# Attention of a decoder trunk: scores of the next pair of heads placed inside the products of this pair, and the output projection split 2, 3, 3 instead of 2, 2, 4

## The chip, the cores and the metric

The kernel runs on one core of a Trainium2 chip. The time is in device microseconds (us) of one execution. The engines work side by side and each carries out its own instructions in a fixed order: PE multiplies matrices and writes its results to eight banks of an accumulator memory (PSUM), DVE does elementwise work and scans, ACT does copies, casts and functions such as the sigmoid, POOL does a little setup, and SP's queue issues the loads. The order on each engine is fixed when the program is built.

## The reference, cut to what matters

A trunk of two layers works on 512 tokens with 16 learned meta tokens in front (528 rows) and a width of 1024. Layer 0 mixes tokens by causal pooling. Layer 1 uses stick-breaking attention with 16 heads of 64. Each mixer is followed by a dense feed-forward part (SwiGLU, width 2816), and a norm ends the trunk. The change is in the attention of layer 1:

```python
def _sb_attend(qs, qpos, kvs, kpos):
    z = jnp.einsum('bqhd,bkhd->bhqk', q, k) * (HEAD_DIM ** -0.5)
    mask = kpos[None, :] < qpos[:, None]
    log_keep = jnp.where(mask, log_sigmoid(-z), 0.0)
    later = lax.cumsum(log_keep, axis=3, reverse=True) - log_keep
    a = jnp.where(mask, exp(log_sigmoid(z) + later), 0.0)
    return jnp.einsum('bhqk,bkhd->bqhd', a, v)

def sb_mixer(h, w_qkv, w_o):
    q, k, v = ...   # h @ w_qkv, in 16 heads
    o = sweep_queries(_sb_attend, (q,), (k, v))
    return o.reshape(B, L, N_HEADS * HEAD_DIM) @ w_o
```

So the weight of a key is sigmoid(z) times the product of sigmoid(-z) over all later keys that the query sees.

## The kernel before, in words

**Precision.** Every float32 product is made of three matmuls (`mm3`, line 102): each operand is split into a high part (a cast on ACT) and a low part (a subtraction on DVE), and high x high, high x low and low x high are added up. `wsplit` (line 82) does that for weights, 512 columns at a time. `wraw` (line 75) loads them through SP's queue into six buffers. The split weights have eight buffers each for high and low.

**Units of the attention.** The 16 heads go in 8 pairs, a pair filling the 128 rows of a tile. For pair p there are these steps:

- `proj(p)` (line 498): five half steps, q (512 columns at once), k in two halves of 264 columns, v in two halves. Each is 24 matmuls. Line 524 scales the result with the norm on DVE, and `parts_of` (line 528) splits q and k.
- `values` (line 535): transposes of v on PE, and their split into `vv`.
- `scores` (line 551): three groups of matmuls `z` with masks added (line 570). Query block 3 goes first, then blocks 0 and 1, then block 2 and the start of block 3. All four causal blocks of the pair's two heads lie in strips of 1344 columns, `sg` and `kp`, of which there is one each. Two sigmoids on ACT (line 573) fill them group by group. Then, for each head, a scan on DVE (line 576) makes the running product from the last key backwards in place, and line 578 multiplies it with `sg`. The second head's two instructions are kept behind the first head's.
- `turned(p, hd)` (line 585): ten transposes of the strip on PE (line 589), one for the meta columns (line 602), then the splits `a1`, `a2` and `a0` on ACT and DVE (lines 607 to 614). `a1` and `a2` have room for one head (high and low), and `a0` is one tile.
- `attend(p, hd)` (line 618): nine matmuls `po` of the weights with `vv`, collected into `of`. `finish(p)` (line 636) splits `of` into `os`.
- `wo(p0, p1)` (line 642): the output projection over pairs p0 to p1 in eight steps, one for each chunk of 128 output columns. A step is a weight split, 3 matmuls of 512 columns for each pair (`pw`), and an addition to the residual stream `hT` on DVE (line 655).

**The loop.** For each pair, lines 664 to 697 write down: the scores of pair p, its `values`, q and the first half of k of pair p+1, the transposes of head 0, the second half of k, the products of head 0, the transposes of head 1, the first half of v, the products of head 1, the second half of v. For pairs 3 to 6 some steps of `wo(0, 2)` follow. Pair 7 has five steps of `wo(2, 4)` in place of projections. The other three stand between the steps of `wo(4, 8)` at the end (line 699), each of which is followed by a chunk of the next feed-forward part's norm.

**What sets the order.** This written order is a priority. The builder (line 777) lays the instructions of each engine on a timeline of its own estimates and takes, at each moment, the first written one that it believes ready and for which a buffer is free. `tc.issue_after(x)` holds every instruction inside it that runs on x's engine behind x. Before, it holds the scores of pair p behind the last product of pair p-1.

**Banks.** In this stage PSUM has four single banks (tag `one`: projections, a part of the transposes, products, output steps, and the norm's sum of `norm_bcast`, line 164, which takes two) and two double banks (tag `two`: scores, the larger part of the transposes, `values`, and for pair 0 also the projections).

Of the kernel before, what the change touches and what calls it, by code (L numbers as in the profile page):

```python
# [7 lines left out]
F32 = mybir.dt.float32  # L8
# [42 lines left out]
def trunk(ctx: ExitStack, tc: tile.TileContext, x, meta, x_t, gain, pool_w, w_qkv, w_o, w_gate, w_up, w_down,  # L51
# [50 lines left out]
    def mm3(outs, wh, wl, xh, xl, start, stop, more=False):  # L102

        for i, (w, xx) in enumerate(((wh, xh), (wh, xl), (wl, xh))):
            for o, sl in outs:
                nc.tensor.matmul(o, lhsT=w, rhs=xx[:, sl], start=start and i == 0, stop=stop and i == 2,  # L106
                                 skip_group_check=more)
# [377 lines left out]
    with tc.tile_pool(name="att", bufs=1) as ap, phase("ps2", one=4, two=2):  # L485
# [12 lines left out]
        def proj(p):  # L498

            got = {}  # L500
            first = {}

            def half(i, hf):
                if hf == 0:
                    got["w"] = wsplit(wraw(w_qkv[i * KC + p], f"r{'qkv'[i]}{p}"), f"w{'qkv'[i]}{p}")
                    got[i] = blk(f"qf{p}_{i}")
                wh, wl = got["w"]
# [43 lines left out]
        def scores(p, q, k):  # L551


            (qh, ql), (kh, kl) = q, k
            sg, kp = (ap.tile([P, 2, STRIP], F32, tag=t, name=f"{t}{p}", bufs=1) for t in ("sg", "kp"))

            for o, n, regs in ((832, 512, ((3, 0, META, L),)), (0, 416, ((0, 0, 0, 144), (1, 144, 0, 272))),
                               (416, 416, ((2, 0, 0, 400), (3, 400, 0, META)))):
                tz = ps(f"z{p}_{o}", "two", 2)
# [7 lines left out]
                for d in DIAG:  # L567
                    if o <= d < o + n:
                        for hd in range(2):
                            nc.tensor.matmul(tz[:, hd, d - o:d - o + P], lhsT=masks[:, 2], rhs=masks[:, 0], start=False,  # L570
                                             stop=True, skip_group_check=True)
                for dst, sc in ((kp, -1.0), (sg, 1.0)):
                    nc.scalar.activation(dst[:, :, o:o + n], tz[:, :, 0:n], AF.Sigmoid, scale=sc)  # L573

            def weights(hd):
# [5 lines left out]
            with tc.issue_after(weights(0)):  # L581
                weights(1)
            return sg[:, 0], sg[:, 1]
# [52 lines left out]
        def finish(p, of):  # L636
            a, b = (ap.tile([P, SEQ], F32R, tag="os", name=f"os{p}{n}", bufs=11) for n in "hl")
            nc.scalar.copy(a, of)
            nc.vector.tensor_tensor(out=b, in0=of, in1=f32(a), op=ALU.subtract)
            osp[p] = (a, b)  # L640

        def wo(p0, p1):
# [4 lines left out]
            def step(c):  # L647
# [5 lines left out]
                for j in range(n):  # L653
                    mm3([(pj, slice(0, SEQ))], wh[j], wl[j], *osp[p0 + j], j == 0, j == n - 1)
                nc.vector.tensor_tensor(out=hT[c][:, TOK], in0=pj, in1=hT[c][:, TOK], op=ALU.add)

            return [lambda c=c: step(c) for c in range(KC)]

        NP = NH // 2
        got, steps, values = proj(0)  # L660
        for st in steps:
            st()
        early = wo(0, 2)
        for p in range(NP):
            of = ap.tile([P, SEQ], F32, tag="of", name=f"of{p}", bufs=1)
            extra = []
            if p < NP - 1:
                nxt, nsteps, nvalues = proj(p + 1)
                before = []
                fill = nsteps[0:1], nsteps[1:2], nsteps[2:3], nsteps[3:4], nsteps[4:]  # L670
                if p == NP - 2:
                    late, fill = nsteps[3:], fill[:3] + ([], [])
                if 3 <= p < NP - 1:
                    extra = early[:4] if p == NP - 2 else early[:2 if p == 3 else 1]
                    early = early[len(extra):]
            else:
                w = wo(2, 4)
                before, fill = late, (w[0:1], w[1:2], w[2:3], w[3:4], w[4:5])
            with tc.issue_after(last) if p else nullcontext():
                s0, s1 = scores(p, got["q"], got["k"])  # L680
            for st in before:
                st()
            values()
            for st in list(fill[0]) + list(fill[1]):
                st()
            w0 = turned(p, 0, s0)
            for st in fill[2]:
                st()
            attend(p, 0, w0, got["v"], of)
            w1 = turned(p, 1, s1)  # L690
            for st in fill[3]:
                st()
            last = attend(p, 1, w1, got["v"], of)
            finish(p, of)
            for st in list(fill[4]) + list(extra):
                st()
            got, values = nxt, nvalues
# [83 lines left out]
```

## Time and profile before

| what | value |
|---|---|
| three runs | 1085.02, 1086.45, 1087.53 us; median 1086.45 |
| the profiled execution | 1087.54 us, of which 1085.6 us is the span of the trace; mean granted PE clock 0.978 |
| PE busy | 1030.8 us (95%) |
| DVE busy | 856.2 us (79%) |
| ACT busy | 558.2 us (51%) |
| attention | from 410.4 us (first q projection) to 723.4 us (last output step) of the span |

PE is busy nearly everywhere. Its clock is shown as a share of full speed, and it can fall to a half, in which case a busy PE does half as much. So a stage has to be read in three columns: PE's busy time, its clock, and what ended its idle time. The attention is the stage in which PE's busy share is lowest: in slices 18 to 26 of the page's 40 it reads 7 to 9 tenths.

### The profile page before, as it was taken

To read this page: it belongs to the slowest core of one execution; us is meant where nothing else is said; L and a number is where in the kernel's file an instruction comes from. 1 tells how busy PE (TensorE), PEld (TensorE's weight loads), DVE (VectorE), ACT (ScalarE), POOL (GpSimd) and SP (SyncE) were. 2 spreads that over 40 slices of the span, in tenths; PEclk is the share of its full clock that TensorE was granted. 3 is DMA by queue.
4 is the path that set the end of the run, shared out by engine and by line. 5 is a ranking of instruction groups with operands and counts; after the bars stand their busy time and mean duration, and the time that the engine had idled before them with its cause. 6 is when DMAs were issued, how large, how long until landed. Compare 5 with 4: busy or idle time off the path is not lost.

```text
span 1085.6 us, 18620 instructions
## 1 busy us (share of the span) xinstructions
PE 1030.8 (95%) x7302; PEld 956.6 (88%) x7302; DVE 856.2 (79%) x1529; ACT 558.2 (51%) x1131; POOL 6.2 (1%) x16
## 2 busy tenths in 40 slices
PE   8998999999999999798888899799999999999997
PEld 6997999999999998787788778678899999999985
DVE  7899987878888685766688768789987777878855
ACT  7555644545444454555554545356664454455544
POOL 1000000000000010000000000000000000000000
PEclk9999999999999999899999999899999999999999
DMA  9112332233232332101110102222233232333312
GB/s 346 65 53 73 133 98 98 98 98 98 98 97 98 117 108 88 39 30 40 49 59 21 49 30 79 78 97 69 77 105 101 98 98 97 108 107 117 98 39 78
DMA packets 43111, 95.72 MB, mean 88 GB/s; under 512 B 3328, under 2 KB 20096, under 8 KB 43024
## 3 DMA queue, kind: packets, MB, share of 16 engines
q1 hardware_dynamic: 42272, 93.40, 25.9%
q8 instruction: 57, 0.93, 0.3%
q10 hardware_dynamic: 752, 1.14, 0.3%
q14 instruction: 30, 0.25, 0.1%
HBM read 92.43 MB, written 2.10 MB: 87 GB/s over the span
## 4 chain that ended last, share of the span: by engine, by line
PE 80%; DVE 15%; ACT 2%; issue 1%; DMA 1%; SPq 0%; ACTq 0%; DVEq 0%
PE pb L106 15%; PE pd L106 11%; PE pd L330 11%; PE pj L106 11%; PE pa L106 10%; PE pc L106 10%; DVE kp L576 3%; PE pw L106 2%; PE po L628 2%; PE pp L106 2%; PE z L564 2%; PE t L589 2%; DVE sg L578 1%; DVE xl L389 1%; ACT kp L573 1%
## 5 line engine op out<-in xcount | busy, mean ns | idle before, releaser
L576 DVE TENSOR_TENSOR_SCAN kp<-kp,estrip 128x1344 f32<-128x1344 f32 x16 | 47.3, 2954 | 21.0 <-ACT kp L573 21.0
L303 DVE TENSOR_TENSOR h<-pd,h 128x264 f32<-128x264 f32 x96 | 41.2, 431 | 13.9 <-PE pd L106 13.9
L92 ACT CAST ws_3h<-rgate 128x512 fp32r<-128x512 f32 x38 | 23.6, 621 | 55.3 <-PE pb L106 49.3
L589 PE MATMUL t<-consts,sg 128*128 128x128 f32 x160 | 26.1, 319 | 25.5 <-DVE sg L578 22.4
L92 ACT CAST ws_5h<-s 128x512 fp32r<-128x512 f32 x38 | 23.6, 621 | 47.0 <-PE pb L106 36.3
L589 PEld LDWEIGHTS t<-consts,sg 128*128 128x128 f32 x160 | 21.7, 163 | 28.1 <-issue 24.2
L106 PE MATMUL pa<-xl,ws_0h 128*128 128x264 f32 (+1 forms) x152 | 43.4, 285 | 3.2 <-DVE xl L389 3.2
L432 DVE TENSOR_TENSOR u<-pb,m 128x264 f32<-128x264 f32 (+1 forms) x38 | 16.3, 430 | 38.1 <-PE pb L106 38.0
L92 ACT CAST ws_4h<-s 128x512 fp32r<-128x512 f32 x38 | 23.6, 621 | 42.3 <-PE pa L106 25.6
L106 PE MATMUL pb<-xl,ws_1h 128*128 128x264 f32 (+1 forms) x152 | 43.1, 284 | 1.0 <-DVE xl L389 1.0
L106 PE MATMUL pc<-xh,ws_2l 128*128 128x264 f32 (+1 forms) x152 | 43.2, 284 | 0.0
L106 PE MATMUL pb<-xh,ws_1h 128*128 128x264 f32 (+1 forms) x152 | 43.2, 285 | 0.0
L106 PE MATMUL pa<-xh,ws_3h 128*128 128x264 f32 (+1 forms) x152 | 43.1, 284 | 0.0
L106 PE MATMUL pa<-xh,ws_0l 128*128 128x264 f32 (+1 forms) x152 | 43.1, 284 | 0.0
L106 PE MATMUL pb<-xh,ws_6l 128*128 128x264 f32 (+1 forms) x152 | 43.1, 283 | 0.0
L106 PE MATMUL pa<-xl,ws_3h 128*128 128x264 f32 (+1 forms) x152 | 43.0, 283 | 0.0
L106 PE MATMUL pb<-xh,ws_4l 128*128 128x264 f32 (+1 forms) x152 | 43.0, 283 | 0.0
L106 PE MATMUL pc<-xl,ws_2h 128*128 128x264 f32 (+1 forms) x152 | 43.0, 283 | 0.0
L106 PE MATMUL pc<-xl,ws_5h 128*128 128x264 f32 (+1 forms) x152 | 43.0, 283 | 0.0
L106 PE MATMUL pb<-xl,ws_6h 128*128 128x264 f32 (+1 forms) x152 | 43.0, 283 | 0.0
L106 PE MATMUL pc<-xh,ws_2h 128*128 128x264 f32 (+1 forms) x152 | 43.0, 283 | 0.0
L106 PE MATMUL pb<-xl,ws_4h 128*128 128x264 f32 (+1 forms) x152 | 43.0, 283 | 0.0
(1179 smaller groups left out, 4177.6 us busy)
## 6 DMA issues: line engine op xcount, KB each, us to landing
rgate<-in_ffn_w_gate_dram SPq DMA_DIRECT2D x44, 512.0 KB, 3.5
rup<-in_ffn_w_up_dram SPq DMA_DIRECT2D x44, 512.0 KB, 3.4
rd<-in_ffn_w_down_dram SPq DMA_DIRECT2D x42, 512.0 KB, 3.6
rq<-in_sb_w_qkv_dram SPq DMA_DIRECT2D x8, 512.0 KB, 3.4
rk<-in_sb_w_qkv_dram SPq DMA_DIRECT2D x8, 512.0 KB, 3.4
rv<-in_sb_w_qkv_dram SPq DMA_DIRECT2D x8, 512.0 KB, 3.5
h<-in_x_t_dram SPq DMA_DIRECT2D x8, 264.0 KB, 6.8
x<-in_x_dram SPq DMA_DIRECT2D x4, 512.0 KB, 5.4
```

What stands on the lines that cost most here:

```text
L92: nc.scalar.copy(hi, v[:, j:j + w])
L106: nc.tensor.matmul(o, lhsT=w, rhs=xx[:, sl], start=start and i == 0, stop=stop and i == 2, skip_group_check=more)
L303: nc.vector.tensor_tensor(out=hv, in0=pd, in1=hv, op=ALU.add)
L330: nc.tensor.matmul(pd, lhsT=hid[j][x_][:, ts], rhs=w_[:, sl], start=r > 0 and i + j == 0, stop=j == len(hid) - 1 and i == 2, skip_group_ch ...
L389: nc.vector.tensor_tensor(out=xl[i][:, m, :], in0=o, in1=f32(xh[i][:, m, :]), op=ALU.subtract)
L432: tt(out=u[:, a], in0=pb, in1=m1, op=ALU.add)
L564: nc.tensor.matmul(tz[:, hd, c:c + k1 - k0], lhsT=qq[hs, i * P:(i + 1) * P], rhs=kk[hs, k0:k1], start=j == 0 and c == 0, stop=False, skip_ ...
L573: nc.scalar.activation(dst[:, :, o:o + n], tz[:, :, 0:n], AF.Sigmoid, scale=sc)
L576: nc.vector.tensor_tensor_scan(kp[:, hd, ::-1], kp[:, hd, ::-1], estrip[:, ::-1], 1.0, op0=ALU.mult, op1=ALU.max)
L578: return nc.vector.tensor_tensor(out=sg[:, hd, 0:STRIP - 1], in0=sg[:, hd, 0:STRIP - 1], in1=kp[:, hd, 1:STRIP], op=ALU.mult).ins
L589: nc.tensor.transpose(o, sg[:, c0:c0 + n], ident)
L628: last = nc.tensor.matmul(po[:, i0 * P:512], lhsT=lw, rhs=a, start=t == 0 and j == 0, stop=t == 4)
```

## The change

The helper `mm3` and the steps now return their last matmul, so that others can be placed behind it. `Scores` is the old `scores` cut into its three groups and the scans. `begin` writes them down with given steps in front and between, each held behind the other on PE. In the loop, pair p+1's scores and scans now stand between the transposes of pair p's second head and that head's products, with half a k of pair p+2 in front of the first two groups and the other half in front of the third; q of pair p+2 follows. Both halves of v of pair p+1 and its `values` stand between the transposes and the products of pair p's first head. Pair 0's scores are written down with its own v around, and q and k of pair 1 follow them before the loop. All projections use single banks. The output projection runs over pairs 0 and 1 (four steps after each of pairs 4 and 5), over pairs 2 to 4 (in place of projections in pairs 6 and 7), and over pairs 5 to 7 at the end. `os` has 10 buffers in place of 11.

```diff
@@ mm3
-                nc.tensor.matmul(o, lhsT=w, rhs=xx[:, sl], start=start and i == 0, stop=stop and i == 2,
-                                 skip_group_check=more)
+                last = nc.tensor.matmul(o, lhsT=w, rhs=xx[:, sl], start=start and i == 0, stop=stop and i == 2,
+                                        skip_group_check=more)
+        return last.ins
@@ proj
-                    got["w"] = wsplit(wraw(w_qkv[i * KC + p], f"r{'qkv'[i]}{p}"), f"w{'qkv'[i]}{p}")
+                    got["w", i] = wsplit(wraw(w_qkv[i * KC + p], f"r{'qkv'[i]}{p}"), f"w{'qkv'[i]}{p}")
...
-                if p == 0:
-                    if hf == 0:
-                        first[i] = ps(f"pj{p}_{i}", "two", 2)
-                    pj = first[i][:, hf, :n]
-                else:
-                    pj = ps(f"pj{p}_{i}{hf}", "one")[:, :n]
+                pj = ps(f"pj{p}_{i}{hf}", "one")[:, :n]
                 for k in range(KC):
-                    mm3([(pj, sl)], wh[k], wl[k], uh[k], ul[k], k == 0, k == KC - 1)
+                    last = mm3([(pj, sl)], wh[k], wl[k], uh[k], ul[k], k == 0, k == KC - 1)
...
+                return last
@@ scores
-        def scores(p, q, k):
...
+        class Scores:
+            GROUPS = ((832, 512, ((3, 0, META, L),)), (0, 416, ((0, 0, 0, 144), (1, 144, 0, 272))),
+                      (416, 416, ((2, 0, 0, 400), (3, 400, 0, META))))
+            def __init__(self, p, q, k):
+                self.p, self.q, self.k = p, q, k
+                self.sg = ap.tile([P, 2, STRIP], F32, tag="sg", name=f"sg{p}", bufs=1)
+                self.kp = ap.tile([P, 2, STRIP], F32, tag="kp", name=f"kp{p}", bufs=1)
+            def group(self, g):
+                (qh, ql), (kh, kl) = self.q, self.k
+                o, n, regs = self.GROUPS[g]
+                tz = ps(f"z{self.p}_{o}", "two", 2)
...
+                for dst, sc in ((self.kp, -1.0), (self.sg, 1.0)):
                     nc.scalar.activation(dst[:, :, o:o + n], tz[:, :, 0:n], AF.Sigmoid, scale=sc)
+                return last.ins
+            def weights(self, hd):
...
+            def both(self):
+                with tc.issue_after(self.weights(0)):
+                    self.weights(1)
@@ finish
-            a, b = (ap.tile([P, SEQ], F32R, tag="os", name=f"os{p}{n}", bufs=11) for n in "hl")
+            a, b = (ap.tile([P, SEQ], F32R, tag="os", name=f"os{p}{n}", bufs=10) for n in "hl")
@@ the loop
+        def begin(p, got, before, between):
+            sc = Scores(p, got["q"], got["k"])
+            mark = None
+            for st in before:
+                mark = st()
+            with tc.issue_after(mark) if mark else nullcontext():
+                sc.group(0)
+                mark = sc.group(1)
+            for st in between:
+                with tc.issue_after(mark):
+                    mark = st()
+            with tc.issue_after(mark):
+                sc.group(2)
+            sc.both()
+            return sc.sg
+
         got, steps, values = proj(0)
-        for st in steps:
+        for st in steps[:3]:
             st()
-        early = wo(0, 2)
+        sg = begin(0, got, [], steps[3:4])
+        steps[4]()
+        values()
+        nxt, steps, values = proj(1)
+        for st in steps[:3]:
+            st()
+        early, w = wo(0, 2), wo(2, 5)
         for p in range(NP):
             of = ap.tile([P, SEQ], F32, tag="of", name=f"of{p}", bufs=1)
...
+            v = got["v"]
+            w0 = turned(p, 0, sg[:, 0])
+            for st in steps[3:] if p + 1 < NP else w[4:6]:
+                st()
+            if p + 1 < NP:
+                values()
+            attend(p, 0, w0, v, of)
+            w1 = turned(p, 1, sg[:, 1])
+            got = nxt
+            if p + 2 < NP:
+                nxt, steps, values = proj(p + 2)
+                fill = steps[1:2], steps[2:3], steps[0:1]
+            elif p + 2 == NP:
+                fill = w[0:1], w[1:2], w[2:4]
             else:
...
+                fill = [], [], w[6:8]
+            if p + 1 < NP:
+                sg = begin(p + 1, got, fill[0], fill[1])
             for st in fill[2]:
                 st()
...
+            attend(p, 1, w1, v, of)
+            if p in (4, 5):
+                for st in early[4 * (p - 4):4 * (p - 3)]:
+                    st()
             finish(p, of)
...
         norms[1] = Norm(24, "f1")
-        for c, st in enumerate(wo(4, NP)):
-            if c < 3:
-                w[5 + c]()
+        for c, st in enumerate(wo(5, NP)):
             st()
             norms[1].chunk(c)
```

More of the change, by code (lines that the diff above doesn't have):

```diff
@@ L500, in proj @@
             got = {}
-            first = {}
             def half(i, hf):
                 if hf == 0:
-                    got["w"] = wsplit(wraw(w_qkv[i * KC + p], f"r{'qkv'[i]}{p}"), f"w{'qkv'[i]}{p}")
+                    got["w", i] = wsplit(wraw(w_qkv[i * KC + p], f"r{'qkv'[i]}{p}"), f"w{'qkv'[i]}{p}")
                     got[i] = blk(f"qf{p}_{i}")
-                wh, wl = got["w"]
+                wh, wl = got["w", i]
                 f = got[i]
@@ L569, in scores @@
                         for hd in range(2):
-                            nc.tensor.matmul(tz[:, hd, d - o:d - o + P], lhsT=masks[:, 2], rhs=masks[:, 0], start=False,
-                                             stop=True, skip_group_check=True)
-                for dst, sc in ((kp, -1.0), (sg, 1.0)):
+                            last = nc.tensor.matmul(tz[:, hd, d - o:d - o + P], lhsT=masks[:, 2], rhs=masks[:, 0],
+                                                    start=False, stop=True, skip_group_check=True)
+                for dst, sc in ((self.kp, -1.0), (self.sg, 1.0)):
                     nc.scalar.activation(dst[:, :, o:o + n], tz[:, :, 0:n], AF.Sigmoid, scale=sc)
-            def weights(hd):
+                return last.ins
+            def weights(self, hd):
+                kp, sg = self.kp, self.sg
                 nc.vector.tensor_tensor_scan(kp[:, hd, ::-1], kp[:, hd, ::-1], estrip[:, ::-1], 1.0, op0=ALU.mult,
@@ L579, in weights @@
                                                in1=kp[:, hd, 1:STRIP], op=ALU.mult).ins
-            with tc.issue_after(weights(0)):
-                weights(1)
-            return sg[:, 0], sg[:, 1]
+            def both(self):
+                with tc.issue_after(self.weights(0)):
+                    self.weights(1)
         def turned(p, hd, sg):
@@ L653, in step @@
                 for j in range(n):
-                    mm3([(pj, slice(0, SEQ))], wh[j], wl[j], *osp[p0 + j], j == 0, j == n - 1)
+                    last = mm3([(pj, slice(0, SEQ))], wh[j], wl[j], *osp[p0 + j], j == 0, j == n - 1)
                 nc.vector.tensor_tensor(out=hT[c][:, TOK], in0=pj, in1=hT[c][:, TOK], op=ALU.add)
+                return last
             return [lambda c=c: step(c) for c in range(KC)]
         NP = NH // 2
+        def begin(p, got, before, between):
[13 more added lines that the diff above has]
+            return sc.sg
@@ L660, in trunk @@
         got, steps, values = proj(0)
-        for st in steps:
+        for st in steps[:3]:
             st()
-        early = wo(0, 2)
+        sg = begin(0, got, [], steps[3:4])
[5 more added lines that the diff above has]
+        early, w = wo(0, 2), wo(2, 5)
         for p in range(NP):
             of = ap.tile([P, SEQ], F32, tag="of", name=f"of{p}", bufs=1)
[L666 to L675, printed above, removed]
-            else:
[L677 to L686, printed above, removed]
```

13 lines of the change are left out of this document (removed).

## The prediction

> **What bounds the kernel now.** I read the page first. The tensor engine (PE) is busy almost all of the span, and one group of its instructions, the transposes of the attention weights on line 589, has nearly all of the engine's listed idle time in front of it, released by DVE's product on line 578.
>
> ```profile
> span 1085.6 us, 18620 instructions
> PE 1030.8 (95%) x7302; PEld 956.6 (88%) x7302; DVE 856.2 (79%) x1529; ACT 558.2 (51%) x1131; POOL 6.2 (1%) x16
> L589 PE MATMUL t<-consts,sg 128*128 128x128 f32 x160 | 26.1, 319 | 25.5 <-DVE sg L578 22.4
> ```
>
> Next I cut the attention stage with the view of busy time by stretch: from the first projection of pair 0 to its first scores, one stretch per pair (first score to next first score), the end of pair 7, and the rest of the output projection up to the matmul that sums the next norm. Columns: stretch, length, busy time of PE, PE's weight loads, DVE, ACT, POOL, granted PE clock, DMA share, GB/s.
>
> ```profile
> core 0: us, PE busy (x) PEld busy (x) DVE busy (x) ACT busy (x) POOL busy (x), PEclk, DMA share, GB/s
> 410.40:433.08 22.68, 22.68 (x138) 20.32 (x139) 13.16 (x23) 8.70 (x15) 0.00 (x0) 1.00 0.27 88
> 433.08:464.90 31.82, 25.99 (x192) 23.94 (x191) 23.26 (x32) 17.07 (x35) 0.00 (x0) 0.89 0.11 37
> 464.90:497.25 32.35, 28.87 (x205) 26.02 (x205) 24.06 (x34) 16.36 (x34) 0.00 (x0) 0.95 0.12 42
> 497.25:529.59 32.34, 27.48 (x206) 24.40 (x205) 24.08 (x34) 16.35 (x34) 0.00 (x0) 1.00 0.12 41
> 529.59:564.73 35.14, 31.66 (x217) 28.14 (x217) 25.96 (x38) 17.39 (x36) 0.00 (x0) 0.95 0.16 48
> 564.73:598.47 33.74, 30.22 (x212) 26.94 (x211) 25.10 (x35) 16.77 (x35) 0.00 (x0) 0.95 0.10 33
> 598.47:632.20 33.73, 30.29 (x212) 27.07 (x211) 24.04 (x34) 16.35 (x35) 0.00 (x0) 0.95 0.14 45
> 632.20:661.95 29.75, 26.17 (x170) 22.29 (x169) 21.65 (x30) 14.23 (x31) 0.00 (x0) 0.94 0.16 53
> 661.95:695.03 33.08, 27.53 (x166) 22.76 (x167) 26.16 (x38) 15.63 (x34) 0.00 (x0) 0.90 0.20 64
> 695.03:732.66 37.63, 36.73 (x158) 29.36 (x158) 28.37 (x46) 19.21 (x33) 0.00 (x0) 1.00 0.30 98
> sum 322.26, PE 287.64 PEld 251.25 DVE 235.84 ACT 158.05 POOL 0.00; mean PE 28.76 PEld 25.12 DVE 23.58 ACT 15.81 POOL 0.00
> ```
>
> PE is idle for 322.26 - 287.64 = 34.6 us. It also loses time to a lower clock: (1 - clock) x length over the rows gives 3.5 + 1.6 + 0 + 1.8 + 1.7 + 1.7 + 1.8 + 3.3 = 15.4 us. So 50.0 us of this part are not matmul work at full clock; 272.3 us are. A pair without output projection needs about 27.4 us of PE (28.87 less 1.6; 27.48 at full clock) and 24.1 us of DVE, and takes 32.35.
>
> The view of waits names the releasers in the attention stage, and the timeline of pair 3 shows the chain: third group of scores, sigmoid on ACT, scan of head 0 on DVE (line 576), two evacuations that DVE puts between, the product (line 578), the transposes.
>
> ```profile
> PE t L589 <- DVE sg L578: 22.4, 8, 5.3
> PE po L628 <- DVE a L614: 5.2, 7, 0.9
> ```
>
> ```profile
> 537.76 0.28 PE L570 MATMUL z<-masks 128*128 128x128 bf16 x2
> 538.08 0.86 ACT L573 ACTIVATE kp<-z 128x832 f32<-128x832 f32 x1 [2.89 <-PE z L570]
> 538.98 2.96 DVE L576 TENSOR_TENSOR_SCAN kp<-kp,estrip 128x1344 f32<-128x1344 f32 x1 [3.06 <-ACT kp L573]
> 541.85 0.67 DVE L524 TENSOR_TENSOR qf<-pj,r 128x512 f32<-128x512 f32 x1
> 542.43 0.81 DVE L546 TENSOR_TENSOR vv<-pv,vv 128x640 fp32r<-128x640 f32 x1
> 543.16 1.55 DVE L578 TENSOR_TENSOR sg<-sg,kp 128x1343 f32<-128x1343 f32 x1
> 544.86 1.59 PE L589 MATMUL t<-consts,sg 128*128 128x128 f32 x10 [2.63 <-DVE sg L578]
> 552.56 1.45 DVE L614 SCALAR_TENSOR_TENSOR a<-a0h,consts,t 32x128 fp32r<-32x128 f32 x4
> 554.06 0.50 PE L628 MATMUL po<-a,vv 128*128 128x512 f32 x1 [0.85 <-DVE a L614]
> ```
>
> From the end of the scores (538.04) to the transposes is 6.8 us, 5.3 without the two evacuations (1.5 us). Until then PE had 4.2 us of projection to do and waited 2.63. Of the wait's other cost the clock tells: stretches of 3.4 us around this place.
>
> ```profile
> 545.70:549.10 3.40, 3.40 (x18) 3.40 (x16) 3.40 (x5) 1.20 (x2) 0.00 (x0) 0.50 0.00 0
> 549.10:552.50 3.40, 3.40 (x28) 3.31 (x28) 3.40 (x5) 2.06 (x8) 0.00 (x0) 1.00 0.47 154
> 513.20:516.60 3.40, 3.40 (x31) 3.40 (x30) 3.40 (x4) 2.07 (x4) 0.00 (x0) 1.00 0.02 5
> ```
>
> After the wait of pair 3 PE runs for 3.4 us at half clock and loses 1.7 us; after the like wait of pair 2 (third row) it does not. Pair 2 alone of pairs 1 to 6 has clock 1.00 in the table.
>
> **The change part by part.** The chain of waits gives PE's pieces at full clock: start, length, and count.
>
> ```profile
> 531.94 4.91 PE pj L106 x21
> 522.21 2.93 PE pj L106 x24
> 525.14 1.51 PE po L628 x9
> 550.97 1.09 PE t L589 x10
> 561.94 2.79 PE pw L106 x12
> ```
>
> So a q projection (24 matmuls of 512 columns, 0.234 each) is 5.6 us, half a k or v projection 2.9, a head's products 1.5, a head's transposes 1.1, and an output step 0.2325 per matmul: 1.4 us for two pairs, 2.1 for three. No matmul is added or removed, so the 272.3 us stay; what changes are the losses. I price them one by one.
>
> *Wait for the first transposes.* After the third group of scores of pair p+1, the new order has q of p+2 (5.6) and the second head's products of pair p (1.5): 7.1 us against a chain of 6.8. That alone leaves no wait. But nothing holds q back, and the builder orders PE by its own estimates. Before, it put 21 q matmuls between the second and third groups (531.94, 4.91 us). The new order puts half a k there (2.9); I let q fill the other 2.0 us, which is 9 matmuls. Then 15 x 0.234 + 1.5 = 5.0 us of cover are left and the wait is between 5.3 - 5.0 = 0.3 and 6.8 - 5.0 = 1.8; I take 1.3, nearer to the upper end, because DVE did put work between in pair 3. Pairs 1 to 4: 5.2 us. Pairs 5 and 6 get four output steps of 1.4 us in front: 0. Pair 7 has two steps of 2.1 and 1.5 of products, 5.7 against 6.8 or 5.3: 0.8. Together 6.0, bounds 0 and 4 x 1.8 + 1.5 = 8.7.
>
> *Wait for the first head's products.* From the start of the transposes to the last split that the products need, DVE took 9.2 us (544.86 to 554.01: scan and product of head 1 and the splits). The new order covers this with transposes 1.1, v 5.9, v's own transposes 0.5 and eight of nine product matmuls 1.3: 8.8. The wait is 0.4 plus what else DVE must do there; I take 0.6 (0.85 before, with a shorter cover), for 7 pairs 4.2; bounds 0 and 7 x 1.5 = 10.5.
>
> *Half clock.* Before, 2.63 us of wait and 1.1 of transposes cost 1.7 us in most pairs. With 1.3 of wait I take one pair in four of five: 2.1; bounds 0 and 7 x 1.7 = 12. The Trainium skill says, in TensorE: Matmul & The Clock Gate, section HAM oscillation — how this bites in real kernels, that the clock falls only with idle gaps above about 3.4 us. By that rule this term would be 0 and the time 2 us less, but this trace halves the clock after 2.63. The same page, section Part 4: PE-mode transpose, says that transposes do not count as busy in the same way; with them the gap is 3.7, and the trace agrees.
>
> *Start.* The pieces of pair 0's q and k move from the double banks to the four single ones, which the norm's sum also takes two of. q, the sum (two) and half of k fill all four, so the second half of k now waits until line 137 has read the sum, and q's bank comes free only later.
>
> ```profile
> 417.14 1.05 PE L172 MATMUL abp<-ansq,ones 128*128 128x264 f32 x4
> 420.36 0.77 DVE L137 SCALAR_TENSOR_TENSOR abt<-abp,abt 128x264 f32<-128x264 f32 x2
> 422.38 0.69 DVE L524 TENSOR_TENSOR qf<-pj,r 128x512 f32<-128x512 f32 x1
> ```
>
> q and half of k are 8.5 us from 410.4, so PE has work to 419 or so and the bank is there at 421.2: 1.5 us with the sum's own matmuls; bounds 0 (the sum goes earlier) and 5 (the bank is given after q, 423.1, and the clock falls). Behind it on PE stand pair 0's scores, and q of pair 1 has no free bank to run ahead in. Pair 0's own wait (5.3 in the waits, clock 0.89) gets v, q and k of pair 1 in front, 2.9 + 5.6 + 5.9, and goes.
>
> *Pair 7.* Its transposes are followed by two output steps (4.2) and eight product matmuls (1.3): 1.1 + 4.2 + 1.3 = 6.6 against 9.2, a wait of 2.6, less since DVE has no projection to split. The second head's splits have 4.2 more. I take 3.5 in all, bounds 1 and 9 (the last stretch of pair 7 loses 5.6 + 3.3 now).
>
> *End.* Output projection regrouped as 2, 3, 3 pairs:
>
> ```profile
> 695.03:732.66 37.63, 28.13 (x120) 22.18 (x119) 8.89 (x13) 1.00 0.30 98
> rwo<-in_sb_w_o_dram SPq DMA_DIRECT2D x8, 256.0 KB, 2.7
> rwo<-in_sb_w_o_dram SPq DMA_DIRECT2D x4, 512.0 KB, 3.4
> ```
>
> The first row is the projection alone in the last stretch: 28.1 us of PE. After it, 8 steps of 2.1 = 16.8 remain there; 11 us move into pairs 5 to 7, where they are the cover counted above. Finishing pair 7 is hidden by the matmuls of pairs 5 and 6 in the first steps. But DVE's 28.4 us in that stretch shrink only by splits made earlier, to 25 or so, while PE has 16.8 + 8.6 = 25.4. Now they are level, so I leave 2.3 us of loss (0.9 now); bounds 0.9 and 8. The loads of `w_o` stay 12 issues on SP's queue, and those of q, k and v only change their order there. Four of 256 KB and eight of 384 KB meet a DMA share of 0.10 to 0.20: nothing. The splits and additions of the projection stay the same in elements: nothing.
>
> *Sum.* 1.5 + 6.0 + 4.2 + 2.1 + 3.5 + 2.3 = 19.6 us of losses for 50.0: 30.4 less. The profiled execution took 1087.54 (1085.6 of span and 1.9 around it), so it would take 1057.1. The median of the runs shown, 1086.45, lies 1.1 lower: **1056**.
>
> **Rivals.** *B, DVE's queue and the banks become the bound.* The second group of scores needs the double bank of head 1's transposes, which DVE frees after the splits of head 1, and these wait for head 0's products. That circle is: transposes to products 9.2, head 1's splits about 3, second group and mask 1.2, k 2.9, third group 1.2, chain 6.8: 24.3 us, 3 under PE's 27.4. For it: DVE has 24.1 us of work a pair and only a part of it is in the circle (about 12). If half of the rest is served in front, the circle is 30.3, the loss 2.9 a pair, and with half clock in some 3.6: 7 x 3.6 + 1.5 + 3.5 + 2.3 = 32.5, 17.5 less: 1069. Against it: DVE idles 8 us a pair now.
>
> *C, the cover is spent early, and it is slower.* If all 24 q matmuls go in front of the third group, only the products' 1.5 us stand between it and the transposes, and the wait is 6.8 - 1.5 = 5.3, as at pair 0, with 6.8 us at half clock there (3.5 in the row of pair 0; 2.8 taken). With 0.85 for the products that is 9.0 a pair for pairs 1 to 4 and 7, 45; 5 and 6 keep 0.6 each; 45 + 1.2 + 1.5 + 3.5 + 2.3 = 53.5, 3.5 more than now: 1090. It decides from about 20 matmuls on. For it: the 21 in the trace. Against: half a k now stands there.
>
> *D, it does not overlap.* The strips for sigmoids and scan results stay single, so pair p+1's sigmoids wait until pair p's are read. If all of DVE's 24.1 us and the circle's 8.3 us on other engines (transposes, copies, scores, k, sigmoid) run one behind the other, the pair takes 32.4 as now; 7 x 5 + 7.3 = 42 of loss: 1078. Against: the transposes that read the strips come 2.9 us of k before. The Trainium skill says, in Perfetto Trace Analysis, section Identifying Performance Opportunities, that a gap that repeats can mean too few buffers; by that rule reordering would leave it. Here the releaser is DVE's product, data and not a bank, so the trace speaks against it.
>
> *E, better.* No waits but the start and the end: 1.5 + 1 + 0.9 = 3.4, 1040; with a little left, 1044.
>
> **How the numbers follow.** Forecast 0.58 (own range 1047 to 1064), B 0.20, E 0.07, D 0.06, C 0.09. The range 1042 to 1076 takes in the forecast, B and most of E; it leaves out D, C and the edge of E, about 0.18. A change of 0.2% (2.2 us) is about what can be told from none. C lies beyond it; the edge of D gives 0.03 to no change: faster 0.88, same 0.03, slower 0.09.
>
> **What would show it.** Right: line 589's waits on line 578 fall from 22.4 us to about 6, none above 2; the pairs without output steps take 28.5 to 29.5 us; few half-clock stretches in the stage; the order of PE shows a part of q between second and third groups; the sum of the next norm starts near 702. Wrong: a wait above 4 us at the transposes in most pairs (C), waits of the second score group for DVE's split on line 611 (B), pairs still at 32 (D), or a gap of several us before pair 0's second half of k.

## The result, and the profile after

The changed kernel takes 1060.96 us (median of 4 runs, 1059.19 to 1062.80) against 1085.94 us for the kernel before, run beside it: a ratio of 0.9771, with a 95% interval of 0.9758 to 0.9784. It is faster by 25 us. The profiled execution of after is the slowest of the four, 1062.80 us with a span of 1061.0, and 24.7 us below the profiled execution of before.

From the page of after: the span, the busy times, and the group of scans. DVE's idle time in front of the scans, 3.8 us here, was 21.0 us before.

```profile
span 1061.0 us, 18586 instructions
PE 1023.1 (96%) x7302; PEld 949.3 (89%) x7302; DVE 856.6 (81%) x1529; ACT 556.9 (52%) x1131; POOL 6.2 (1%) x16
L581 DVE TENSOR_TENSOR_SCAN kp<-kp,estrip 128x1344 f32<-128x1344 f32 x16 | 47.3, 2954 | 3.8 <-ACT kp L576 3.4
```

The stage by stretch, in the columns of the prediction. The cuts are the first score of each pair; the first row is pair 0's projection, the last runs from pair 7's last products to the sum of the next norm.

```profile
core 0: us, PE busy (x) PEld busy (x) DVE busy (x) ACT busy (x) POOL busy (x), PEclk, DMA share, GB/s
408.83:423.12 14.29, 12.67 (x76) 11.22 (x76) 10.25 (x19) 7.31 (x13) 0.00 (x0) 1.00 0.20 73
423.12:459.74 36.62, 36.61 (x273) 33.98 (x273) 25.28 (x35) 18.36 (x36) 0.00 (x0) 0.95 0.21 72
459.74:488.70 28.96, 27.61 (x204) 24.48 (x205) 24.84 (x35) 16.42 (x33) 0.00 (x0) 1.00 0.16 56
488.70:517.68 28.98, 27.72 (x204) 24.56 (x204) 24.28 (x34) 16.38 (x33) 0.00 (x0) 1.00 0.11 37
517.68:546.65 28.97, 27.74 (x203) 24.57 (x203) 24.27 (x34) 16.38 (x33) 0.00 (x0) 1.00 0.16 55
546.65:574.93 28.28, 27.47 (x203) 24.57 (x203) 23.40 (x34) 15.27 (x33) 0.00 (x0) 1.00 0.12 39
574.93:608.98 34.05, 33.03 (x229) 28.94 (x229) 28.37 (x42) 17.60 (x37) 0.00 (x0) 1.00 0.19 59
608.98:642.33 33.35, 32.17 (x212) 27.45 (x213) 27.83 (x42) 18.31 (x38) 0.00 (x0) 1.00 0.20 67
642.33:674.28 31.95, 28.36 (x151) 23.27 (x152) 25.74 (x36) 14.18 (x30) 0.00 (x0) 0.89 0.15 50
674.28:705.76 31.48, 27.33 (x106) 21.75 (x106) 22.38 (x36) 16.47 (x28) 0.00 (x0) 0.89 0.25 84
sum 296.93, PE 280.71 PEld 244.79 DVE 236.64 ACT 156.68 POOL 0.00; mean PE 28.07 PEld 24.48 DVE 23.66 ACT 15.67 POOL 0.00
```

The stage is 25.3 us shorter (322.26 before). PE is idle for 296.93 - 280.71 = 16.2 us and loses (1 - clock) x length = 1.8 + 3.5 + 3.5 = 8.8 us, 25.0 together for 50.0. The matmul work is 280.71 - 8.8 = 271.9 us, as before (272.3). (Where PE is idle inside a half-clock stretch, this counts the time twice, about 1 us in either kernel.) A pair without output projection takes 28.97 us for 32.35, with PE idle 1.2 to 1.4 us in pairs 1 to 3. The losses that are left sit in the first two rows and the last two.

PE's waits in the stage (total, times, longest) give them names:

```profile
PE pp L106 <- DVE h L660: 4.1, 1, 4.1
PE t L594 <- DVE sg L583: 3.6, 1, 3.6
PE z L567 <- ACT qk_1h L527: 1.6, 1, 1.6
PE po L633 <- DVE a L619: 1.0, 3, 0.4
```

The wait of the transposes (line 594 now) for DVE's product was 22.4 us in 8 waits; one is left, at pair 7. In the pairs before it the chain is covered, as the timeline of pair 2 shows: last mask of the third score group, scan, product, and the transposes without a wait.

```profile
495.02 0.28 PE L573 MATMUL z<-masks 128*128 128x128 bf16 x2
495.11 0.48 PE L106 MATMUL pj<-anuh,wq3h 128*128 128x512 f32 x1
496.41 2.96 DVE L581 TENSOR_TENSOR_SCAN kp<-kp,estrip 128x1344 f32<-128x1344 f32 x1
499.47 1.56 DVE L583 TENSOR_TENSOR sg<-sg,kp 128x1343 f32<-128x1343 f32 x1
500.75 0.39 PE L633 MATMUL po<-a111h,vv 128*128 128x512 f32 x1
502.25 1.25 PE L594 MATMUL t<-consts,sg 128*128 128x128 f32 x10
```

All of pair 3's q (495.11 to 500.75, 5.6 us) and the products of pair 1's second head (1.5) stand behind the third group. The chain ends at 501.03, 1.2 us before PE comes to the transposes.

At pair 7 the cover is spent early. Of the two output steps that are to follow the third group, one and a third stand in front of it, beside the one meant to (644.56 to 649.6), and 2.9 us of work are left for the chain, up to 653.9:

```profile
654.71 0.67 DVE L660 TENSOR_TENSOR h<-pw,h 128x512 f32<-128x512 f32 x1
...
655.76 1.55 DVE L583 TENSOR_TENSOR sg<-sg,kp 128x1343 f32<-128x1343 f32 x1
657.45 2.36 PE L594 MATMUL t<-consts,sg 128*128 128x128 f32 x10 [3.59 <-DVE sg L583]
```

At the end PE has finished the output projection at 691.0, and the first matmul of the next layer waits for DVE's last residual addition, which stands behind splits and chunks of the norm. By the kernel's text this matmul reads only the first chunk of the norm; but the next layer takes a new set of PSUM banks, and that addition is the last to read the old set:

```profile
693.65 0.76 DVE L153 SCALAR_TENSOR_TENSOR f1ul<-h,gains,f1uh 128x528 fp32r<-128x528 f32 x1
694.33 0.68 DVE L660 TENSOR_TENSOR h<-pw,h 128x512 f32<-128x512 f32 x1
695.16 0.77 PE L106 MATMUL pp<-f1uh,wgate0h 128*128 128x512 f32 x1 [4.15 <-DVE h L660]
```

### The profile page after: what moved, and what is told of

It is laid out like the page before. It is cut to its first block, busy times and chain, and to the rows that moved or that the text cites. A ratio compares the mean times of both kernels' runs of the same rounds, so it can differ in the third digit from the quotient of the medians.

```text
span 1061.0 us, 18586 instructions
## 1 busy us (share of the span) xinstructions
PE 1023.1 (96%) x7302; PEld 949.3 (89%) x7302; DVE 856.6 (81%) x1529; ACT 556.9 (52%) x1131; POOL 6.2 (1%) x16
## 4 chain that ended last, share of the span: by engine, by line
PE 78%; DVE 17%; issue 2%; ACT 1%; DMA 1%; SPq 0%; ACTq 0%; DVEq 0%
PE pb L106 15%; PE pd L106 11%; PE pd L331 11%; PE pa L106 10%; PE pc L106 10%; PE pj L106 9%; PE pp L106 4%; DVE kp L581 2%; PE pw L106 2%; PE z L567 2%; DVE xl L390 1%; DVE a L619 1%; PE t L594 1%; DVE t L387 1%; DVE sg L583 1%
## 5 line engine op out<-in xcount | busy, mean ns | idle before, releaser
L106 PE MATMUL pa<-xh,ws_3l 128*128 128x264 f32 (+1 forms) x152 | 43.3, 285 | 0.0
L106 PE MATMUL pa<-xh,ws_0h 128*128 128x264 f32 (+1 forms) x152 | 43.1, 284 | 0.0
L106 PE MATMUL pb<-xh,ws_1l 128*128 128x264 f32 (+1 forms) x152 | 42.9, 283 | 0.0
L106 PE MATMUL pc<-xh,ws_5h 128*128 128x264 f32 (+1 forms) x152 | 42.9, 282 | 0.0
```

Of the source, the lines that this page charges most:

```text
L106: last = nc.tensor.matmul(o, lhsT=w, rhs=xx[:, sl], start=start and i == 0, stop=stop and i == 2, skip_group_check=more)
```

## The experiments

All are edits of the changed kernel, but for the one on the regrouping alone. Each was timed in three rounds against the kernel before, the last three in five.

**Where q stands.** The theory: what stands behind the third score group decides whether PE waits. The rival: the circle of double banks and DVE's queue (the prediction's B) sets the pair.

```diff
-                fill = steps[1:2], steps[2:3], steps[0:1]
+                fill = steps[1:2], steps[2:3] + steps[0:1], []
```

> All 24 matmuls of the next but one pair's q (5.6 us) are put between the second and third score groups, behind half a k, for pairs 1 to 6; nothing is left out. Theory (what stands behind the third group decides): the transposes of pairs 1 to 4 have only the second head's products, 1.5 us, in front of them against a chain of 5.3 to 6.8 us, so PE waits 3.8 to 5.3 us there and loses about 1.7 to 3.4 more at half clock; the pair grows from 29.0 to 34 us or more, the time rises by 20 to 30 us against the changed kernel, to 1081 to 1091 (the prediction's rival C says 1090). Pairs 5 and 6 keep four output steps and stay. Rival (the circle of double banks and DVE's queue sets the pair, and q's place does not): the pair stays under 30.5 us and the time under 1068.

Measured: 1089.97 us, ratio to before 1.0034 (1.0020 to 1.0049). The whole gain is gone and 0.3% more. The waits, and the stretches behind the first two of them:

```profile
PE t L594 <- DVE sg L583: 22.5, 5, 4.8
```

```profile
475.50:482.30 6.80, 4.79 (x22) 4.82 (x23) 6.77 (x6) 2.21 (x6) 0.00 (x0) 0.50 0.00 0
...
509.60:516.50 6.90, 4.81 (x23) 4.84 (x24) 6.87 (x6) 2.21 (x6) 0.00 (x0) 0.51 0.00 0
```

There are four waits of 4.8 us (the fifth, 3.1, is pair 7's). The last 2.0 to 2.5 us of each and the 4.3 to 4.8 us of work behind it run at half clock. The waits of the stage are back to their 22 us of before. The overlap alone, with all scores and scans still made a pair ahead, gains nothing without the cover in its place.

**The order that the prediction assumed.** It let 9 of the 24 q matmuls go in front of the third group. This run makes that order, by splitting q's step in two and holding the second part behind the third group.

```diff
-                fill = steps[1:2], steps[2:3], steps[0:1]
+                fill = steps[1:2], steps[2:3] + steps[5:6], steps[6:7]
...
+                lambda: half(0, 0, range(3)), lambda: half(0, 0, range(3, KC))]
...
             for st in fill[2]:
-                st()
+                with tc.issue_after(mark) if p + 2 < NP else nullcontext():
+                    st()
```

> The order that the prediction assumed: 9 of the 24 q matmuls stand between the second and third score groups, the other 15 are held behind the third, for the q of pairs 2 to 7; nothing is left out. The run with all 24 in front waits 4.84 us with 1.5 us of cover, so a chain of 6.3. Theory (the chain is fixed, and each matmul moved behind the third group takes 0.234 us off the wait): 15 x 0.234 + 1.5 = 5.0 us of cover, 1.3 us of wait in pairs 1 to 4 and little half clock; 5 to 8 us over the changed kernel, 1066 to 1069. Rival (as DVE gets other work in the chain, the wait does not follow the cover): below 0.6 us or above 2.5 us a pair, 1062 to 1064 or over 1074.

Measured: 1072.36 us, ratio 0.9871 (0.9856 to 0.9886); 11 to 12 us over the changed kernel, outside both expectations. The waits, the row of one pair, and its two waits (the second is in the next pair's scores):

```profile
PE t L599 <- DVE sg L588: 7.7, 5, 3.6
PE z L572 <- DVE vv L546: 5.0, 5, 1.5
```

```profile
507.45:538.27 30.82, 27.83 (x204) 24.52 (x204) 24.25 (x34) 16.54 (x34) 0.00 (x0) 1.00 0.11 35
```

```profile
507.45 1.28 PE L599 MATMUL t<-consts,sg 128*128 128x128 f32 x10 [1.07 <-DVE sg L588]
524.59 0.51 PE L572 MATMUL z<-qk_1h,qk_0h 64*128 64x144 f32 x4 [1.53 <-DVE vv L546]
```

The wait at the transposes is 1.07 us where the cover's arithmetic gave 1.3: that theory holds. But the pair is 1.85 us longer (30.82 for 28.97), because a second wait stands beside the first: the second score group needs the double bank of v's transposes, which DVE frees late, 1.53 us. In the changed kernel the only wait of the score groups is 0.5 us, for a split of head 1. So double banks that DVE frees late, the rival's circle, do cost time, here at v's bank and not at head 1's. Why DVE is late there is not settled. Its chain ends 1.1 us after PE is ready for the transposes, and that may carry on; but the builder also moved v's last transposes on PE, from 3.2 us in front of the scores (514.51 for 517.68) to 0.8 us (521.10 for 521.88), so the edit changed more than q's place. By the cuts of the stage table, pairs 2 to 4 take 32.33 (with a half-clock stretch), 30.82 and 31.27 us, 8.2 us more than in the changed kernel; pairs 5 and 6 take 2.8 more.

**Pair 7's fill held back.**

```diff
             with tc.issue_after(mark):
-                sc.group(2)
+                mark = sc.group(2)
...
             for st in fill[2]:
-                st()
+                with tc.issue_after(mark):
+                    st()
```

> The work that fills the chain is held behind the third score group in program order as well; in the order of instructions this moves only pair 7's output steps, 4.2 us of them, from before the third group to behind it. Nothing is left out. Theory (the 3.6 us wait of pair 7 and its half clock come from the cover spent early): 4.2 + 1.5 = 5.7 us then stand against a chain of 5.3 to 6.8, the wait falls to about 1 us and the half clock behind it goes (3.4 us), 4 to 6.5 us less than the changed kernel: 1054.5 to 1057. Rival (DVE's residual additions and weight splits in the chain make the wait, wherever the steps stand): the wait stays above 2.5 us and the time within 2 us of the changed kernel's.

Measured: 1058.71 us, ratio 0.9744 (0.9726 to 0.9762), 2.3 us under the changed kernel, though the intervals overlap and the time lies above the theory's 1054.5 to 1057. In the trace the wait is what the theory said, and a part of the gain is taken back by the products, which wait for DVE's splits instead:

```profile
PE po L633 <- DVE a L619: 2.0, 4, 1.0
PE t L594 <- DVE sg L583: 1.0, 2, 0.8
```

The waits for the scan's product are 0.8 and 0.2 us now for 3.6, and the half clock in the pair is gone. But the products of pair 7 now wait 0.5 and 1.0 us for DVE's splits, so PE's idle time in the pair falls only from 3.6 to 2.5 us: behind the removed wait DVE's own work sets the pace. From the first score to the last product, pair 7 takes 29.16 us; it took 31.95 in the profiled execution of the changed kernel and 30.90 in a second trace of that kernel (the run without edits in the last set below), where one half-clock stretch and not two follows the same 3.59 us wait. So the edit is worth 1.7 to 2.8 us there, as the time says; the 2.6 us of wait and 3.5 of half clock that it takes away on paper priced it too high.

**The grouping of the output projection.** The changed kernel with 2, 2 and 4 pairs (its edit is shown), and the old loop with 2, 3 and 3 (the opposite edit in the kernel before, `wo(2, 5)` and `wo(5, NP)`):

```diff
-        early, w = wo(0, 2), wo(2, 5)
+        early, w = wo(0, 2), wo(2, 4)
...
-        for c, st in enumerate(wo(5, NP)):
+        for c, st in enumerate(wo(4, NP)):
```

> The changed kernel with the output projection grouped 2, 2, 4 as before; nothing is left out. Theory (the regrouping takes PE work away from the end, where DVE then sets the pace): with 8 steps of 2.8 us PE has 22.3 us there and DVE's additions keep up, so the 4.1 us wait at the end of the stage and most of the half clock behind it go, 4 to 7 us back; pair 7's two fills shrink from 4.2 to 2.8 us each and its waits grow by 1 to 3 us. Net 1 to 6 us faster than the changed kernel, 1055 to 1060. Rival (the prediction's: regrouping pays, as the moved 5.6 us are cover in pair 7 and the end is level): 3 to 7 us slower than the changed kernel, 1064 to 1068.

> The kernel before, its loop unpipelined, with the output projection alone regrouped as 2, 3, 3; nothing is left out. Theory (the 25 us come from the pipelining, the regrouping moves its work only where DVE waits take it back): within 3 us of the kernel before, 1083 to 1089. Rival (a good part of the gain is the regrouping's, as PE's last stretch gets 5.6 us shorter and pairs 6 and 7 get the work as cover): 4 to 8 us faster than the kernel before, 1078 to 1082.

Measured: 1061.03 us, ratio 0.9766 (0.9745 to 0.9787), for the first, the same as the changed kernel and between its two expectations; 1085.28 us, ratio 0.9993 (0.9983 to 1.0004), for the second, the same as before. So the whole gain is the pipelining's. The waits of the first say why the grouping moves nothing:

```profile
PE t L594 <- DVE sg L583: 4.1, 1, 4.1
PE z L567 <- DVE vv L542: 2.2, 2, 2.1
PE pp L106 <- DVE h L660: 2.1, 1, 2.1
```

The wait at the end is 2.1 us for 4.1 and has no half clock behind it, but the shorter steps leave a wait of 2.1 us at pair 7's scores and one of 4.1 at its transposes, each followed by a half-clock stretch. Work moved from the end into pair 7 buys there what it costs at the end.

**The start.** Two runs. The first gives pair 0's q and k their double banks back, since the prediction saw a loss in single ones. The second puts the first half of pair 0's v in front of its first scores.

```diff
+            first = {}
...
-                pj = ps(f"pj{p}_{i}{hf}", "one")[:, :n]
+                if p == 0 and i < 2:
+                    if hf == 0:
+                        first[i] = ps(f"pj{p}_{i}", "two", 2)
+                    pj = first[i][:, hf, :n]
+                else:
+                    pj = ps(f"pj{p}_{i}{hf}", "one")[:, :n]
```

```diff
-        sg = begin(0, got, [], steps[3:4])
+        sg = begin(0, got, steps[3:4], [])
```

> Pair 0's q and k are put into the two double banks as before the change; nothing is left out. Theory of the prediction (the start loses to a bank that the norm's sum holds): the gap of 1.6 us ahead of pair 0's first scores and the half clock behind it (1.7 us) go, 2 to 3.5 us less than the changed kernel. Rival (the trace of after: k runs through without a gap, and the wait is for ACT's and DVE's split of k, behind which nothing else is ordered): the gap stays at 1.3 to 2 us, the time within 1.5 us of the changed kernel's.

> The first half of pair 0's v (2.9 us) is put ahead of pair 0's first scores, where the changed kernel has it between the second and third group; nothing is left out. Theory (the 1.6 us gap there is ACT's and DVE's split of k with nothing ordered behind k): the gap goes, with it the stretch of half clock behind it (1.7 us), and pair 0's third group loses a cover that it does not need: 2 to 3.5 us less than the changed kernel, 1057.5 to 1059. Rival (the norm's chain on DVE sets when pair 0 gets on, and the gap only moves): within 1 us of the changed kernel.

Measured with double banks: 1065.04 us, ratio 0.9807 (0.9786 to 0.9828), 4 us slower than the changed kernel. Both expectations missed. The second half of k now waits for DVE to read its first half out of the same double bank, and DVE reads it only after the norm's sum:

```profile
423.23 0.42 DVE L525 TENSOR_TENSOR qf<-pj,abr 128x264 f32<-128x264 f32 x1
423.71 0.59 PE L106 MATMUL pj<-anuh,wk0h 128*128 128x264 f32 x1 [3.44 <-DVE qf L525]
```

With v's half in front: 1061.08 us, ratio 0.9774 (0.9756 to 0.9793), no change. In its trace the 1.6 us wait and the half clock behind it are gone, and from the first projection to pair 1's first score it takes 49.14 us; the changed kernel takes 50.84 (408.83 to 459.67).

```profile
409.51:458.65 49.14, 48.23 (x347) 43.76 (x347) 35.95 (x55) 26.02 (x48) 0.00 (x0) 1.00 0.24 75
```

The 1.7 us are less than three runs can tell, so this one is inconclusive; the theory's 1057.5 to 1059 was missed.

**The end.** DVE's norm chunks 2 to 7 are ordered behind the last residual addition (`step` returns that addition in place of its last matmul).

```diff
-            st()
-            norms[1].chunk(c)
+            last = st()
+            if c < 2:
+                norms[1].chunk(c)
+        for c in range(2, KC):
+            with tc.issue_after(last):
+                norms[1].chunk(c)
```

> DVE's part of the next norm's chunks 2 to 7 is ordered behind the last residual addition; nothing is left out. Theory (the 4.1 us at the end are PE waiting for that addition, which stands on DVE behind 2.2 us of the norm's chunks and one split): the wait falls to 2 us or less and the half clock behind it to one stretch or none, 2 to 5 us less than the changed kernel, 1056 to 1059. Rival (DVE is busy without a break from 681 to 701 us and its sum for the norm, not PE, sets the end): the wait falls but the norm's sum stays at its time, and the time falls by less than 1.5 us.

Measured: 1059.03 us, ratio 0.9754 (0.9735 to 0.9772), 1.9 us less than the changed kernel, though the intervals overlap here too.

```profile
PE pp L106 <- DVE h L660: 1.5, 1, 1.5
```

The wait falls to 1.5 us and the half clock goes (the clock is 1.00 from 690.92 to 706.41), as the theory has it. The norm's sum is no earlier (296.6 us after the first projection, 296.8 in the changed kernel), as the rival has it: PE's earlier start goes into matmuls of the next layer (1880 in that stretch for 1853) that it then needn't do later. The time lies at the edge of the first expectation.

**Together.** First all three edits, then in one set the changed kernel itself, the two edits on pair 7 and the end, and all three again.

> Three edits on the changed kernel at once: the fill held behind the third score group, the first half of pair 0's v ahead of its first scores, and the norm's chunks behind the last residual addition. Nothing is left out. If their gains add, 2.3 for the first as measured and 2 to 3.5 and 2 to 5 for the others: 1050 to 1055. If the end is set by DVE's sum for the norm and the start by the norm's chain: 1057 to 1059, as with the first alone.

> The changed kernel once more, unedited, as the measure for the next two on the same chip: 1059 to 1063.

> Two edits on the changed kernel: the fill held behind the third score group and the norm's chunks behind the last residual addition. Nothing is left out. If the two are independent, their single gains (2.3 and 1.9) add up: 1056 to 1057.5. If the half clock that the one takes away falls on the other's waits, 1058 to 1060.

> The two edits with, in addition, the first half of pair 0's v ahead of its first scores; nothing is left out. If that third edit is worth nothing, as its own run had it, the same as with two, 1056 to 1057.5; if the 1.7 to 2.3 us that the trace of its own run shows up to the end of the projection are real, 1054 to 1056.

| edits | time, us | ratio to before |
|---|---|---|
| all three | 1056.79 | 0.9739 (0.9716 to 0.9762) |
| none, the changed kernel | 1059.96 | 0.9766 (0.9743 to 0.9788) |
| pair 7 and the end | 1058.46 | 0.9738 (0.9722 to 0.9754) |
| all three, again | 1056.57 | 0.9727 (0.9712 to 0.9742) |

All three beat both the kernel before and the changed kernel: 3.4 us under the changed one in the same set, and the slowest of their eight runs (1058.72) lies beside the fastest of the changed kernel's nine (1058.71). The run of the first row fell between its expectation's two spans. The single gains of 2.3 and 1.9 did not show as a sum with two edits: 1058.46 is in the second expectation's span, but the half clock that this names as the cause is not found behind either edit's place in that trace. What the edit at the start adds, 1.9 us by the medians, is within the intervals and stays open. The traces show why it is hard to see: both runs with it reach pair 1's first score 1.7 us sooner (49.15 us for 50.85 with two edits), and both lose 1.6 us of it again to a half-clock stretch in pair 7 that the run with two edits escapes.

## Why the prediction was right, and where not

The time came out 5 us over the forecast of 1056 and inside the forecast's own range. The mechanism was right: PE's work stayed as it was, and the waits of the transposes went. But no row of its sum was right: pairs 1 to 6 lost 4.0 us less than it said, and the start, pair 7 and the end 9.4 us more, so a part of the nearness is luck. Measured terms are PE's idle time by row of the stage table plus (1 - clock) x length. (The 0.6 us for the products was taken for pairs 0 to 6.)

| place | predicted, us | measured, us |
|---|---|---|
| start, pair 0 | 1.5 + 0.6 = 2.1 | 1.6 + 1.8 = 3.4 |
| pairs 1 to 6: transposes, products, half clock | 5.2 + 3.6 + 2.1 = 10.9 | 6.9 |
| pair 7 | 0.8 + 3.5 = 4.3 | 3.6 + 3.5 = 7.1 |
| end | 2.3 | 4.1 + 3.5 = 7.6 |
| sum | 19.6 | 25.0 |

*Wait for the first transposes.* The step that failed is "I let q fill the other 2.0 us, which is 9 matmuls". No q matmul went in front of the third group, and pairs 1 to 6 have no such wait. The prediction's other sentence, 7.1 us of cover against a chain of 6.8, was the right one. With the assumed order the wait is 1.07 us, within the bounds given (0.3 to 1.8). But that order costs 1072 us, not 1056: the sum had no term for the next place where DVE is late, the score groups' banks, which it had only as rival B. For its own order the forecast was 16 us too low, about 7 of them in pairs 1 to 6 (17.6 us lost there for 10.9) and about 7 in the start, pair 7 and the end; the error in the order hid the first part.

*The signs it gave.* The pairs without output steps take 28.3 to 29.0 us, about as said (28.5 to 29.5). A part of q between the second and third groups and no wait above 2 us did not come (the one left is 3.6 us), and the sum of the next norm starts at 705.6, not near 702.

*Products.* 0.6 us a pair was taken; the waits for line 619 are 0.35 us in pairs 1 to 3 and 1.0 in all. The rest of what PE idles in these pairs, 1.2 to 1.4 us, lies at v's transposes (0.36) and a score group (0.5), for which the sum had no term.

*Half clock.* One pair in four of five was predicted; pairs 1 to 6 have none, since no wait in them is above 0.6 us. All 8.8 us of it stand behind the three long waits of the start, pair 7 and the end, for which the prediction's values hold little or nothing. (The second trace of the changed kernel has one stretch where this one has two, and is 1.05 us shorter in pair 7 and 1.1 at the end. So a stretch cost less than the 1.7 us that (1 - clock) x length gives, and the measured rows are somewhat too high.)

*Start.* The step that failed is "the second half of k now waits until line 137 has read the sum". k runs through without a gap: line 138, which reads the sum now, starts at 417.81, and the second half of k begins at 418.30, right behind the first. The 1.6 us are the wait of the first scores for the split of k. The single banks are a gain of 4 us over double ones in this order, where the prediction had them as a loss of 1.5.

*Pair 7.* The step "two steps of 2.1 and 1.5 of products, 5.7 against 6.8 or 5.3" counted on both steps behind the third group, and the order put one and a third of them in front. That is rival C's mechanism at one pair. The run with the steps held back has the 0.8 us that was predicted for the transposes.

*End.* "Now they are level" compared DVE's and PE's sums over the stretch. They are level in sum (22.4 and 27.3 less 3.5), but the last addition is not last in DVE's work: 4.1 us of wait and 3.5 of half clock come of its place in the queue, and the run that moves it shows that. The price given to the regrouping, 11 us of cover for 1.4 us at the end, is zero by two runs.

*Rivals.* C was priced at 1090 us and its order measured 1089.97. The mechanism is shown: 4.8 us of wait (5.3 taken) and 2.2 to 2.4 of half clock (half of the work done in it; 2.8 taken) in each of pairs 1 to 4. That the total agrees so closely is luck: pairs 5 and 6 of that run lost 10.1 us where C had 1.2, and pair 7 lost 5.5 where it had 12.5. B is there in small. D is refuted: the pair takes 28.97 us. E would need the start, pair 7 and the end, where 18 of the 25 us lie.

## What to carry to other kernels

When work is overlapped with a latency chain, count the work that stands behind the chain's start in the actual order, not the work that is free: here 5.6 us of matmuls on the one side or the other of one score group were worth 29 us. Pin the cover behind the chain's start explicitly if an order is left to a builder, above all in the last iteration, where the filler is of another kind. And price a wait together with what may follow it: in these runs a second wait for the same engine, and the clock behind it.

## What the runs showed of the clock

The prediction could not say why pair 3 of before lost 1.7 us to the clock and pair 2, with a like wait, did not. In every trace the half-clock stretches start and end on a grid of 3.41 us, fixed within one execution (only the last stretch, around the execution's end, ends off it). What goes with a half clock is PE's idle time within one frame of that grid. Two frames of before, pair 2's wait and then pair 3's with the frame behind it:

```profile
508.16:511.57 3.41, 1.71 (x15) 1.49 (x13) 3.41 (x4) 0.91 (x2) 0.00 (x0) 1.00 0.00 0
511.57:514.98 3.41, 2.47 (x22) 2.50 (x23) 3.41 (x2) 1.59 (x5) 0.00 (x0) 1.00 0.02 5
542.29:545.70 3.41, 0.84 (x8) 0.87 (x9) 3.41 (x4) 1.19 (x5) 0.00 (x0) 1.00 0.00 0
545.70:549.11 3.41, 3.41 (x18) 3.41 (x16) 3.41 (x5) 1.21 (x2) 0.00 (x0) 0.50 0.00 0
```

Pair 2's wait lies across two frames with 1.7 and 0.9 us idle, and nothing follows. Pair 3's lies in one, 2.6 us idle, and the next frame runs at half clock. The same two short waits of the products in pair 7 (0.48 and 0.98 us) are parted by a boundary with the fill held back, which cuts the first of them, and fall into one frame with all three edits:

```profile
663.90:667.30 3.40, 2.22 (x9) 1.71 (x10) 3.29 (x8) 1.29 (x4) 0.00 (x0) 1.00 0.01 2
667.30:670.70 3.40, 3.40 (x17) 2.77 (x16) 3.27 (x9) 1.03 (x2) 0.00 (x0) 1.00 0.46 154
```

```profile
660.50:663.90 3.40, 1.95 (x12) 1.47 (x11) 3.29 (x9) 1.36 (x3) 0.00 (x0) 0.99 0.00 0
663.90:667.30 3.40, 3.40 (x10) 2.63 (x9) 3.30 (x8) 0.77 (x2) 0.00 (x0) 0.51 0.47 149
```

Idle 1.2 us in the frame: full clock behind it; idle 1.45: half. Counted over the 14 traces of this case, from 20 to 1040 us of each, frames at full clock, with 1.91 us idle or more, were followed by half clock in 49 of 49 cases; with 1.24 to 1.9 us in 25 of 55; with 0.9 to 1.23 us in 1 of 42. The Trainium skill, in TensorE: Matmul & The Clock Gate, section HAM oscillation — how this bites in real kernels, asks for a gap above about 3.4 us; here no single gap need be that long, and 1.45 us in two pieces was enough.

The way back is sharper. A frame at half clock with 0.39 us idle or less was followed by full clock in 79 of 79 cases, and one with 0.64 us or more by another at half clock in 26 of 26. So how far a wait reaches into a frame decides how long the half clock lasts. The two traces of the changed kernel show it. The first frame at half clock behind pair 7's 3.59 us wait has 0.78 us idle in the profiled execution and 0.30 in the second trace; these are the frames behind it:

```profile
660.08:663.50 3.42, 3.42 (x10) 2.64 (x9) 3.36 (x4) 1.22 (x3) 0.00 (x0) 0.50 0.00 0
```

```profile
661.22:664.63 3.41, 3.41 (x17) 2.73 (x16) 3.38 (x4) 1.49 (x4) 0.00 (x0) 1.00 0.00 0
```

Half clock does not quite halve the work: matmuls of 512 columns follow each other every 0.427 us there (660.04, 660.47, 660.89 in the profiled execution) for 0.234 at full clock.

What blurs the middle band stays open. Counting the transposes as idle, as the prediction did for pair 3, does not sharpen it: the best single threshold puts 29 frames on the wrong side, and 18 when they count as busy. The modelled ends of matmuls may be a cause. Since the frames' phase differs from one execution to the next, the same wait costs one stretch in one and two in another. That fits the 2 to 6 us by which runs of one kernel differ: of the nine executions of the changed kernel, the six with a mean clock of 0.987 or more took 1058.7 to 1061.0 us, and the three below it 1061.5 to 1064.4.
